# Seven block products for pairs of pooled gates, the layer input normalised again in place, and sums of weights formed by DMA

## Chip, core and metric

The kernel runs on one core of a Trainium2 chip. The metric is the device time of one execution in microseconds; several executions are taken and their median stands for the kernel. The engines of the core are TensorE (PE, the matmuls; PEld is its weight load), VectorE (DVE), ScalarE (ACT), GpSimd (POOL) and SyncE (SP), which issues most DMAs. Each engine works through its own queue in order; semaphores tie the queues together.

## What is computed

A decoder trunk with two layers (`DEPTH = 2`), 512 tokens and 16 learned meta tokens ahead of them (528 in all), model width 1024, in float32. Per layer, cut from the reference:

```python
h = rmsnorm(h_res, norm_gain[l])
proj = h @ w_in[l]
u_pool, z_pool, c_q, c_kv, k_rope, z_mla, g_pool, g_mla = jnp.split(proj, IN_SPLIT_POINTS, axis=-1)
y_pool = (pool_mix(u_pool, pool_w_group[l], pool_scale[l]) * jax.nn.silu(z_pool)) @ pool_w_up[l]
o_mla = mla(c_q, c_kv, k_rope, pos, ...)                 # 8 heads, causal, rotary parts, QK-norm
y_mla = (o_mla * jax.nn.silu(z_mla)) @ mla_w_up[l]
merged = jax.nn.sigmoid(g_pool) * y_pool + jax.nn.sigmoid(g_mla) * y_mla
h_res = h_res + merged @ w_out[l]
```

The change concerns `g_pool`, the pooled gate: a product of h (528 x 1024, in the last layer only the 512 tokens count) with 1024 columns of `w_in`, and beside it `g_mla` and `z_mla`, products of the same h.

## The kernel before

All activations lie transposed: channels on the 128 partitions, tokens in the columns. Each float32 product is made of three float32r matmuls on split operands (high x high, high weight x low input, low weight x high input), in `mm3` (L184 to L187). A split is a copy on ACT (high part) and a subtraction on DVE (low part): L276 and L277 for activations, L180 and L181 for weights.

**The stream of products.** `register` (L909) lists all products of a layer as `Gemm`s in order; `stream` (L193) runs through them in chunks of 512 weight columns (4 k-blocks), and has four chunks in preparation: the load by SP into `raw` (3 buffers), then `whi` and `wlo` (3 buffers each). In layer 0 a chunk serves two halves of 264 tokens, 24 matmuls; in layer 1 one piece of 512, 12 matmuls. Results come to PSUM (four buffers `mm`) and are evicted by the `ev_` functions.

**Order.** The list's order around the change: latent queries `cq`, pooled branch `u`, `zp`, `y`, heads' queries `qr`, `qn`, pooled projection `pu` (8), silu gate `zm` (4), pooled gate `gp` (8), attention's gate `gm` (8), attention's projection `mu` (8), output `o` (8). `go` (L973) sets what happens between: `qk_stats` forms the norms of queries (with the Newton steps of L283 to L290 and the factors `nqs`, L685), then the eight heads run. Each `head` (L715) makes scores (PSUM `S`, three buffers), a masked minimum on DVE (`top`, L730; the last of a head combines two halves, L764), exponentials on ACT (L737), and a normalisation on POOL (L774, L776); `pv` transposes and multiplies with the values (L796 to L802). `prep` (L694) makes the next head's key: a multiplication on DVE (L701) and one on POOL (L702), then a split; SP moves the rotary part of the query. Between these parts `gap` (L970) lets the stream advance by `FILL` ns of matmul time as the kernel counts it, until the product named in `RESERVE` is done: `pu`, `zm`, `gp`, and `gm` up to `gm5` fill PE between the attention tiles. The instruction order of each engine is then fixed by a scheduler at build time.

**Normalisation.** `split_h` (L332) splits x times the gain, without the token's factor 1/rms; that factor (`inv`, tile `rinv`) is multiplied in by each eviction: `ev_gp` (L570 to L577), `ev_gm` (L868 to L875), `ev_silu` (L499 to L509) for `zp` and `zm`. The split input stands in 16 tiles `hh`, `hl` all layer long. The tables of the rotary angles (`tcos`, `tsin`) stand in two tiles of their own.

Of the kernel before, what the change touches and what calls it, by code (L numbers as in the profile page):

```python
# [52 lines left out]
FILL = (2950.0, 2850.0)  # L53
RESERVE = ("gm5", "gm5")
# [17 lines left out]
def trunk(ctx, tc, xT, pos, win, wkr, wqb, wkb, wvb, wgr, wpu, wmu, wout, gains, const, yT):  # L72
# [81 lines left out]
    tcos = cp.tile([P, T], F32, name="tcos")  # L154
    tsin = cp.tile([P, T], F32, name="tsin")
# [6 lines left out]
    class Gemm:  # L162
        def __init__(self, name, src, width, evac=None, xs=None, segs=None, body=None, gain=None):
            self.name, self.src, self.width, self.alloc = name, src, width, mmt
            self.evac, self.xs, self.segs, self.body, self.gain = evac, xs, segs, body, gain
            self.spare = False

# [16 lines left out]
    def mm3(out, wh, wl, xh, xl, start, stop):  # L184
        pe.matmul(out, wh, xh, start=start, stop=False)  # L185
        pe.matmul(out, wh, xl, start=False, stop=False)  # L186
        newest[0] = pe.matmul(out, wl, xh, start=False, stop=stop)  # L187
# [5 lines left out]
    def stream():  # L193
# [3 lines left out]
        def load(i):  # L197
            g_, c = flat[i]
            n = min(512, g_.width - c)
            return wload(g_.src[:, c:c + n], n, g_.gain, g_.spare)  # L200
# [73 lines left out]

    def split(hi, lo, src, a, b):
        act.activation(hi[:, a:b], src, AF.Copy)  # L276
        dve.tensor_sub(lo[:, a:b], src, hi[:, a:b].bitcast(F32))  # L277
# [14 lines left out]
    def tables():  # L292
# [7 lines left out]
        dve.tensor_scalar(ang, ang, 3.1415925, -3.1415925, op0=ALU.min, op1=ALU.max)  # L300
        act.activation(tcos, ang, AF.Sin, scale=0.5)
        act.activation(tsin, ang, AF.Sin)
        dve.tensor_mul(tcos, tcos, tcos)
        dve.tensor_scalar(tcos, tcos, -2.0, 1.0, op0=ALU.mult, op1=ALU.add)

# [3 lines left out]
    kdr = [dp.tile([H, T], F32, name=f"kdr{l}") for l in range(DEPTH)]  # L309

    hbuf = [(slot(f"hh{k}", F32R), slot(f"hl{k}", F32R)) for k in range(8)]

    class Layer:
        def __init__(self, l):
            self.l, self.last = l, l == DEPTH - 1
            self.XS = XTOK if self.last else FULL
            self.x0 = NM if self.last else 0
            self.xt = xt if l == 0 else [None] * 8
# [7 lines left out]
            self.sq = []  # L326
            self.st = self.acc = self.inv = self.cinv = self.kraw = self.kp = None
# [154 lines left out]
        def rope(self, out, src, a, b):  # L482
# [3 lines left out]
            dve.tensor_mul(t[:, :n], t[:, :n], tsin[:, a:b])  # L486
            gp.tensor_mul(src, src, tcos[:, a:b])
# [11 lines left out]
        def ev_silu(self, dst, tag, m):  # L499
            def ev(ps, a, b):  # L500
                if a == self.x0:
                    dst[m] = slot(f"{tag}{m}") if tag == "u" else xb[:, m]
# [6 lines left out]
            return ev  # L509

# [59 lines left out]
        def ev_gp(self, m):  # L570
            def ev(ps, a, b):
                t = tmp()
                dve.tensor_mul(t[:, :b - a], ps, self.inv[:, a:b])
                act.activation(t[:, :b - a], t[:, :b - a], AF.Tanh, scale=0.5)
                dve.scalar_tensor_tensor(out=self.am[m][:, a:b], in0=t[:, :b - a], scalar=1.0,
# [534 lines left out]
```

## Time and profile before

| | us |
|---|---|
| median of 3 runs | 789.78 (789.15 to 790.03) |
| profiled execution, span from first to last instruction | 787.1 |
| busy in it: PE / DVE / ACT / POOL | 780.9 / 535.1 / 410.8 / 194.4 |
| layer 0's statistics of queries and keys on PE end (time in the span) | 155.0 |
| first scores of layer 0's head 1 | 190.2 |
| layer 1's statistics end | 550.6 |

The profile is of one execution. Line numbers are those of the kernel. A row of a view that groups instructions gives the line, the engine, the operation, output and inputs with their shapes, the count, then busy time in us and the mean of one in ns, then the engine's idle time before them and what ended it. A row of a timeline gives start and duration in us. A row by stage gives the stretch, its length, the busy time of each engine with the number of instructions, the granted clock of PE, the busy share of the DMA engines and GB/s.

### The profile page before, as it was taken

Reading aid. Unit: us, or ns where it says so; the run is one execution under the profiler, and the core shown is the slowest. Engines: PE = TensorE matmul, PEld = TensorE weight load, DVE = VectorE, ACT = ScalarE, POOL = GpSimd, SP = SyncE. Lnnn points to the kernel's source line nnn. Section 1 sums busy time; section 2 is a strip of 40 time slices with the busy share of each in tenths; the row PEclk is TensorE's granted clock in tenths of the full one; section 3 lists DMA queues with packets and bytes.
Section 4 is the critical chain, followed back from the end, with each engine's and each line's share of the span. In section 5 each row is a group of like instructions: output and inputs, shape, how many; then the busy total and the mean of one; then the engine's idle time right before and its main releaser. Section 6 shows DMA issues by size and latency. Waiting matters only on the chain.

```text
span 787.1 us, 14567 instructions
## 1 busy us (share of the span) xinstructions
PE 780.9 (99%) x5301; PEld 708.6 (90%) x5301; DVE 535.1 (68%) x1165; ACT 410.8 (52%) x930; POOL 194.4 (25%) x259
## 2 busy tenths in 40 slices
PE   9999999999999999999999999999999999999998
PEld 8999899999999999999997898887788888887887
DVE  5848787446779987675464487775467888755932
ACT  7645655635656565633354356455445666554420
POOL 1034504002333242051000145131022333410500
PEclk9999999999999999999999999999999999999999
DMA  6242333423223212224642422334232222122372
GB/s 242 82 102 85 96 120 102 128 81 94 96 76 92 78 58 78 95 81 146 192 123 94 95 88 90 129 88 136 96 105 88 95 84 82 65 81 67 102 242 84
DMA packets 52263, 81.83 MB, mean 104 GB/s; under 512 B 8784, under 2 KB 17360, under 8 KB 52192
## 3 DMA queue, kind: packets, MB, share of 16 engines
q1 hardware_dynamic: 52048, 80.65, 32.9%
q8 instruction: 41, 0.67, 0.4%
q14 instruction: 30, 0.25, 0.1%
q10 hardware_dynamic: 144, 0.26, 0.1%
HBM read 74.49 MB, written 4.27 MB: 100 GB/s over the span
## 4 chain that ended last, share of the span: by engine, by line
PE 95%; DMA 2%; DVE 1%; issue 1%; ACT 0%; SPq 0%; ACTq 0%
PE mm L185 28%; PE mm L187 28%; PE mm L186 28%; PE mm L796 2%; PE S L186 2%; PE S L187 1%; PE S L185 1%; PE o L802 1%; PE o L801 1%; PE S L453 1%; DMA xb<-xT 1%; PE mm L355 1%; DVE wlo L181 1%; PE mm L412 0%; DMA rinv<-win 0%
## 5 line engine op out<-in xcount | busy, mean ns | idle before, releaser
L185 PE MATMUL mm<-hh,whi 128*128 128x264 f32 (+2 forms) x1096 | 346.7, 318 | 0.2 <-ACT racc L810 0.2
L186 PE MATMUL mm<-hl,whi 128*128 128x264 f32 (+2 forms) x1096 | 343.9, 315 | 0.0
L187 PE MATMUL mm<-hh,wlo 128*128 128x264 f32 (+2 forms) x1096 | 343.0, 315 | 0.0
L181 DVE TENSOR_TENSOR wlo<-raw,whi 128x512 fp32r<-128x512 f32 (+2 forms) x251 | 188.6, 755 | 119.6 <-ACT whi L180 115.9
L180 ACT ACTIVATE whi<-raw 128x512 fp32r<-128x512 f32 (+2 forms) x251 | 150.4, 601 | 187.5 <-PE mm L186 126.5
L185 PEld LDWEIGHTS mm<-hh,whi 128*128 128x128 f32 x1096 | 205.9, 188 | 13.6 <-ACT racc L810 0.5
L186 PEld LDWEIGHTS mm<-hl,whi 128*128 128x128 f32 x1096 | 206.6, 189 | 11.8
L187 PEld LDWEIGHTS mm<-hh,wlo 128*128 128x128 f32 x1096 | 205.5, 188 | 12.0
L774 POOL TENSOR_TENSOR pm<-pa,rs 128x16 f32<-128x16 f32 x32 | 11.6, 361 | 181.3 <-DVE rs L769 181.3
L560 POOL TENSOR_TENSOR racc<-racc,tmp 128x264 f32<-128x264 f32 (+1 forms) x15 | 14.2, 948 | 153.8 <-ACT tmp L559 129.8
L702 POOL TENSOR_TENSOR tmp<-kp,bc 64x528 f32<-64x528 f32 x16 | 22.5, 1408 | 76.9 <-PE mm L675 44.5
L884 POOL TENSOR_TENSOR tmp<-tmp,xb 128x264 f32<-128x264 f32 (+1 forms) x24 | 27.1, 1149 | 58.2 <-DVE tmp L882 33.1
L730 DVE CUSTOM_DVE_ANT_0 S<-S,maskw,nqs 128x272 f32<-128x272 f32 (+4 forms) x80 | 38.5, 498 | 4.2 <-PE S L187 3.9
L737 ACT ACTIVATE cq<-S,bia 128x400 f32<-128x400 f32 (+2 forms) x48 | 24.6, 516 | 22.6 <-DVE bia L764 12.0
L185 PE MATMUL mm<-u,whi 128*128 128x264 f32 (+1 forms) x108 | 35.2, 326 | 0.0
L187 PE MATMUL mm<-cq,wlo 128*128 128x264 f32 (+1 forms) x108 | 34.5, 323 | 0.7 <-DVE wlo L181 0.7
L187 PE MATMUL mm<-u,wlo 128*128 128x264 f32 (+1 forms) x108 | 34.8, 323 | 0.0
L185 PE MATMUL mm<-cq,whi 128*128 128x264 f32 (+1 forms) x108 | 34.6, 320 | 0.0
L186 PE MATMUL mm<-cq,whi 128*128 128x264 f32 (+1 forms) x108 | 34.5, 321 | 0.0
L277 DVE TENSOR_TENSOR tl<-mm,th 128x512 fp32r<-128x512 f32 (+1 forms) x64 | 29.3, 481 | 6.1 <-ACT th L276 5.1
L776 POOL TENSOR_TENSOR cq<-cq,rs 128x384 f32<-128x384 f32 (+1 forms) x32 | 32.8, 1025 | 0.0
L186 PE MATMUL mm<-kn,whi 128*128 128x264 f32 (+1 forms) x96 | 30.7, 321 | 0.0
(252 smaller groups left out, 1362.4 us busy)
## 6 DMA issues: line engine op xcount, KB each, us to landing
raw<-win SPq DMA_DIRECT2D x143, 256.0 KB, 2.6
raw<-wout SPq DMA_DIRECT2D x32, 256.0 KB, 2.7
bc<-kdr SPq DMA_DIRECT2D x16, 264.0 KB, 3.6
raw<-wpu SPq DMA_DIRECT2D x16, 256.0 KB, 2.7
raw<-wmu SPq DMA_DIRECT2D x16, 256.0 KB, 2.5
raw<-wqb SPq DMA_DIRECT2D x12, 256.0 KB, 2.6
tmp<-xT SPq DMA_DIRECT2D x16, 132.0 KB, 3.0
tmp<-scr SPq DMA_DIRECT2D x7, 256.0 KB, 3.4
```

The source lines that it names most:

```text
L180: act.activation(hi[:, :n], raw[:, :n], AF.Copy)
L181: dve.tensor_sub(lo[:, :n], raw[:, :n], hi[:, :n].bitcast(F32))
L185: pe.matmul(out, wh, xh, start=start, stop=False)
L186: pe.matmul(out, wh, xl, start=False, stop=False)
L187: newest[0] = pe.matmul(out, wl, xh, start=False, stop=stop)
L277: dve.tensor_sub(lo[:, a:b], src, hi[:, a:b].bitcast(F32))
L702: gp.tensor_mul(kf[r0:r0 + 64, :], self.kp[r0:r0 + 64, :], bc[r0:r0 + 64, :])
L730: dve.tensor_tensor_reduce(out=sv, in0=sv, in1=mask, scale=nqs[:, i, h:h + 1], scalar=3e38, op0=ALU.add, op1=ALU.min, accum_out=bia[:, c:c ...
L737: act.activation(pv, sv, AF.Exp, scale=-1.0, bias=bia[:, i:i + 1], accum_out=rs[:, c:c + 1])
L776: gp.tensor_mul(pt[i][:, NM:], pt[i][:, NM:], rs[:, i:i + 1].to_broadcast([P, n - NM]))
L796: pe.transpose(tr[:, P * (i - j):P * (i - j + 1)], pt[i][:, NM + P * j:NM + P * (j + 1)], ident)
L884: gp.tensor_add(t[:, :b - a], t[:, :b - a], self.am[m][:, a:b])
```

## The change

Pairs of pooled gates are computed by seven block products instead of eight (a scheme of Strassen's kind, in Winograd's form): the 1024 inputs are halved into k-blocks 0 to 3 and 4 to 7, the tokens into two halves, the two gates of a pair are the two column blocks. `fast` makes seven products of 4 k-blocks for one half of the tokens, and its evictions add and subtract them. For this:

- `renorm` replaces the split input by the split of x times gain times `inv`, after the queries are done, so that the products give the gate without a factor; `ev_gm` and `ev_zm` lose their multiplication by `inv` (the factor 0.5 of `zm` moves to where it is used). It is called at eight points of `qk_stats`, 1500 ns of stream apart, in place of one filling of 9500.
- `mixed` forms four sums of halves of the input in place and splits them; its 16 calls stand at four places of each head, 8 of them do something.
- `weight_sums` copies weight blocks from HBM to HBM (`wsum`) on SP and adds others on top by accumulating DMAs that GpSimd issues; `stream` loads the sums like weights. Ten calls stand before head 0 and in heads 0 to 3.
- In the list, pairs `gp0` to `gp3` stand among `gm0` to `gm7`; `FILL` is 2770 and 2700 (2950 and 2850), `RESERVE` is `gp3`.
- For room, the first six `gm` gates are stored to HBM and loaded again (`gates_again`), and so are the rotary tables.

```diff
-FILL = (2950.0, 2850.0)
-RESERVE = ("gm5", "gm5")
+FILL = (2770.0, 2700.0)
+RESERVE = ("gp3", "gp3")
...
-    tcos = cp.tile([P, T], F32, name="tcos")
-    tsin = cp.tile([P, T], F32, name="tsin")
+    tab = [slot("tc"), slot("ts")]
...
+        def renorm(self, k):
...
+            f = self.f[k] = slot("sv", bufs=2) if k % 4 == 3 else slot(f"cq{k}")
+            f, (hh, hl), x0 = f[:, self.x0:T], self.hs[k], self.x0
+            x = xb[:, k, x0:T]
+            if k < 4:
+                sp.dma_start(f, scr[:, k, :] if self.last else xT[:, k, :])
+                x = f
+            behind(dve.scalar_tensor_tensor(out=f, in0=x, scalar=self.g(G_H + k), in1=self.inv[:, x0:T],
+                                            op0=ALU.mult, op1=ALU.mult), newest[0])
+            split(hh, hl, f, self.x0, T)
+
+        def mixed(self, i):
+            k, s = divmod(i, 2)
+            if k > 3:
+                return
+            (a, b), (_, c) = self.XH
+            n = b - a
+            u, w = self.f[k], self.f[k + 4]
+            if s == 0:
+                dve.tensor_sub(w[:, b:c], u[:, b:c], w[:, b:c])
+                dve.tensor_sub(u[:, b:c], u[:, a:b], u[:, b:c])
+                dve.tensor_sub(u[:, a:b], u[:, a:b], w[:, b:c])
+                dve.tensor_sub(w[:, a:b], w[:, a:b], u[:, a:b])
+                return
...
+            split(th, tl, u[:, a:c], a, c)
+            for h_, l_, v in ((t3h, t3l, w[:, b:c]), (t4h, t4l, w[:, a:b])):
+                split(h_, l_, v, 0, n)
...
+        def fast(self, name, a, b, u, got):
+            order = (1, 6, 7, 5, 2, 4, 3)
...
+            src = {1: a[:, 0:512], 2: a[:, 512:1024], 4: b[:, 512:1024], 5: s[:, 0, :], 6: s[:, 1, :], 7: s[:, 2, :],
+                   3: s[:, 3, :]}
...
+                for k in range(4):
+                    xh, xl = (x[:, t[0]:t[1]] for x in self.hs[k + o]) if p < 4 else self.tt[k][p]
+                    c = P * k
+                    mm3(ps, w[0][:, c:c + P], w[1][:, c:c + P], xh, xl, k == 0 and p not in (2, 4, 3), k == 3, True)
...
+                if p == 1:
+                    act.activation(d, ps, AF.Copy)
+                elif p == 6:
+                    dve.tensor_sub(d, d, ps)
+                elif p == 7:
+                    dve.tensor_sub(v, ps, d)
+                elif p == 5:
+                    dve.tensor_sub(v, v, ps)
+                    got(2 * u + 1, B, v, v)
+                elif p == 2:
+                    got(2 * u, A, ps, tmp()[:, :n])
+                elif p == 4:
+                    x = tmp()[:, :n]
+                    dve.tensor_sub(x, ps, d)
+                    got(2 * u + 1, A, x, x)
+                else:
+                    dve.tensor_add(d, d, ps)
+                    got(2 * u, B, d, d)
...
+        def weight_sums(self, i, w):
+            l = self.l
+            u, s = divmod(i, 2)
+            if u < 4:
+                a, b = w[2 * u], w[2 * u + 1]
+                d = wsum[l][u]
+                if s == 0:
+                    for i, t in enumerate((b[:, 0:512], a[:, 0:512], a[:, 0:512], a[:, 512:1024])):
+                        behind(sp.dma_start(d[:, i, :], t), newest[0])
+                else:
+                    for i, t in ((0, b[:, 512:1024]), (2, b[:, 0:512])):
+                        behind(gp.dma_start(d[:, i, :], t, accum_op=ALU.add), newest[0])
+            if 0 < u < 5:
+                d = wsum[l][u - 1]
+                behind(gp.dma_start(d[:, 3 if s else 1, :], d[:, 1 if s else 0, :], accum_op=ALU.add), newest[0])
...
-            fill_now(9500)
+            start = clk[0]
+            for i, k in enumerate((4, 5, 6, 7, 0, 1, 2, 3)):
+                self.renorm(k)
+                fill_to(start + 1500 * (i + 1))
...
-                    self.gms[m] = slot(f"cq{m}")
-                d = self.gms[m][:, a:b]
-                dve.tensor_mul(d, ps, self.inv[:, a:b])
-                act.activation(d, d, AF.Tanh, scale=0.5)
+                    self.gms[m] = slot(f"cq{m}" if m > 5 else "ts" if m % 2 else "tc")
+                act.activation(self.gms[m][:, a:b], ps, AF.Tanh, scale=0.5)
+                if m < 6 and b == T:
+                    sp.dma_start(gate[self.l][:, m, self.x0:T], self.gms[m][:, self.x0:T])
...
-            for m in range(8):
-                add(f"gp{m}", wi(MT_GP + m), D, evac=self.ev_gp(m), xs=hs, segs=XS)
-            for m in range(8):
-                add(f"gm{m}", wi(MT_GM + m), D, evac=self.ev_gm(m), xs=hs, segs=XS)
+            for e in ("gm0", "gp0", "gm1", "gm2", "gp1", "gm3", "gm4", "gp2", "gm5", "gp3", "gm6", "gm7"):
+                m = int(e[2])
+                if e[:2] == "gp":
+                    self.fast(e, wi(MT_GP + 2 * m), wi(MT_GP + 2 * m + 1), m, self.got_gp)
+                else:
+                    add(e, wi(MT_GM + m), D, evac=self.ev_gm(m), xs=hs, segs=XS)
...
-            fill_now(2600)
+            bit()
             kq = self.prep(0)
             fill_now(2600)
+            bit()
...
             for h in range(H):
-                kn_ = self.head(h, kq, prev)
+                kn_ = self.head(h, kq, prev, lambda: self.mixed(next(mix)))
                 self.gap()
+                self.mixed(next(mix))
+                bit()
                 if h + 1 < H:
                     kq = self.prep(h + 1)
                 self.pv(prev, (2, 3))
+                bit()
+                self.mixed(next(mix))
                 prev = kn_
                 self.gap()
+                self.mixed(next(mix))
...
             self.pv(prev, (2, 3))
+            up("gm6")
+            self.gates_again()
             up("gm7")
```

More of the change, by code (lines that the diff above doesn't have):

```diff
@@ L273, in fill_now, with fill_to @@
             pass
+    def fill_to(end):
+        while clk[0] < end and step():
+            pass
     def split(hi, lo, src, a, b):
@@ L755, in head @@
             self.gap()
+            between()
             self.pv(prev, (0, 1))
@@ L975, in go, with bit @@
             up = lambda name: upto((l, name))
+            made, mix = iter(range(99)), iter(range(99))
+            def bit():
+                i = next(made)
+                if i < 10:
+                    self.weight_sums(i, [win[l, MT_GP + m] for m in range(8)])
             if l == 0:
```

108 lines of the change are left out of this document (84 added, 24 removed).

## The prediction

> **What bounds the kernel now.** I read the page first (span, engines, chain), then rows of TensorE's timeline, then busy time by stage, then VectorE's instructions by form.
>
> ```profile
> span 787.1 us, 14567 instructions
> ...
> PE 780.9 (99%) x5301; PEld 708.6 (90%) x5301; DVE 535.1 (68%) x1165; ACT 410.8 (52%) x930; POOL 194.4 (25%) x259
> PEclk9999999999999999999999999999999999999999
> ...
> PE 95%; DMA 2%; DVE 1%; issue 1%; ACT 0%; SPq 0%; ACTq 0%
> ```
> The page: TensorE (PE) is busy for 780.9 of 787.1 us, its clock is granted in full in all slices, and 95% of the chain that ended last is PE. So the time follows the number of matmuls and what one costs, as long as nothing keeps them waiting. The span is 787.1 us; the runs' median, 789.78 us, lies 2.7 us above it, and I keep that difference.
>
> How far apart matmuls start, in timeline rows (start, duration): layer 0's merge (59 rows from the first to the last), layer 1's output projection (36 rows), and its last tile in 256-column halves (41 rows).
>
> ```profile
> 344.83 0.28 PE L186 MATMUL mm<-kn,whi 128*128 128x264 f32 x1
> ...
> 351.90 0.28 PE L187 MATMUL mm<-q,wlo 128*128 128x264 f32 x1
> ```
>
> ```profile
> 739.81 0.39 PE L185 MATMUL mm<-hh,whi 128*128 128x512 f32 x1
> ...
> 747.89 0.39 PE L186 MATMUL mm<-hl,whi 128*128 128x512 f32 x1
> ```
>
> ```profile
> 778.78 0.28 PE L186 MATMUL mm<-hl,whi 128*128 128x256 f32 x1
> ...
> 783.51 0.28 PE L187 MATMUL mm<-hh,wlo 128*128 128x256 f32 x1
> ```
> 58 steps in 7.07 us are 121.9 ns for 264 columns; 35 in 8.08 us are 230.9 ns for 512; 40 in 4.73 us are 118.3 ns for 256. The 0.28 and 0.39 us are latencies that overlap.
>
> The engine with the next least room is VectorE (DVE). By stage (columns: stretch, its length, then busy time of PE, PE's weight loads, DVE, ACT, POOL), the heads of layer 0:
>
> ```profile
> 190.00:320.00 130.00, 130.00 (x1062) 128.50 (x1061) 106.14 (x258) 77.07 (x199) 42.51 (x68) 1.00 0.25 79
> ```
> 106.14 of 130 us: 82%, in the stage into which the change puts its work.
>
> **The change: what PE saves.** A pair of pooled gates was, per layer 0, 2 tiles x 8 k-blocks x 3 x 2 halves = 96 matmuls of 264 columns; seven block products of 4 k-blocks x 3 are 84. Over four pairs that is 48 x 121.9 ns = 5.9 us. In layer 1 it was 2 x 8 x 3 = 48 of 512 columns, and becomes 84 of 256: 4 x (48 x 230.9 - 84 x 118.3) ns = 4.6 us. Sum: **10.4 us** off PE, if nothing waits. No other matmul is added or lost.
>
> **What VectorE gets.** Durations by form (count, then busy us, mean ns):
>
> ```profile
> L181 DVE TENSOR_TENSOR wlo<-raw,whi 128x512 fp32r<-128x512 f32 x223 | 175.0, 787 | 111.5 <-ACT whi L180 110.0
> ...
> L277 DVE TENSOR_TENSOR kl<-tmp,kh 128x528 fp32r<-128x528 f32 x16 | 11.6, 726 | 4.9 <-ACT kh L276 4.8
> ...
> L338 DVE SCALAR_TENSOR_TENSOR hl<-xb,gn,hh 128x528 fp32r<-128x528 f32 x15 | 10.9, 764 | 4.0 <-ACT hh L336 4.0
> ...
> L575 DVE SCALAR_TENSOR_TENSOR xb<-tmp,xb 128x264 f32<-128x264 f32 x16 | 7.3, 457 | 0.8 <-ACT tmp L574 0.8
> ...
> L573 DVE TENSOR_TENSOR tmp<-mm,rinv 128x264 f32<-128x264 f32 x16 | 6.7, 424 | 0.3
> ```
> I take 0.79 us for a 512-wide low part of a weight, 0.73 for a 528-wide one, 0.76 for a 528-wide scaling, 0.44 for anything of 264. Per layer: `renorm` adds 8 scalings and 8 low parts (8 x 1.49 = 11.9); `mixed` adds 16 subtractions of 264 and low parts of 4 x 528 and 8 x 264 (7.0 + 2.9 + 3.5 = 13.4); products use a weight chunk for half as many columns, so 28 chunks instead of 16 (12 x 0.79 = 9.5); the pair's evictions are 9 instructions instead of 8 (1.8); the gates `gm` lose their multiplication by `inv` (16 x 0.44 = 7.0) and `zm` one of two (3.5). Sum for layer 0 about 26 us, for layer 1 much the same: about 52 us on 535. That is hidden only where DVE has room.
>
> **The stretch where it has none: layer 0, from the statistics to head 1's scores.** In the trace DVE sums the statistics from 155.48, takes head 0's last minimum (L764) at 186.55, and PE starts head 1's scores at 190.16:
>
> ```profile
> 155.48 0.89 DVE L464 TENSOR_TENSOR tmp<-S,tmp 8x264 f32<-8x264 f32 x2 [1.30 <-ACT tmp L463]
> 156.84 0.71 DVE L277 TENSOR_TENSOR kl<-tmp,kh 128x528 fp32r<-128x528 f32 x1 [0.47 <-ACT kh L276]
> 157.95 0.69 DVE L181 TENSOR_TENSOR wlo<-raw,whi 128x512 fp32r<-128x512 f32 x1 [0.40 <-ACT whi L180]
> ...
> 183.05 0.43 DVE L505 SCALAR_TENSOR_TENSOR u<-mm,rinv 128x264 f32<-128x264 f32 x1
> ...
> 186.55 0.15 DVE L764 TENSOR_TENSOR bia<-bia 128x1 f32<-128x1 f32 x1
> ```
>
> ```profile
> 190.16 0.29 PE L185 MATMUL S<-kh,qhl 128*128 128x272 f32 x1
> ```
>
> ```profile
> 155.48:186.55 31.07, 31.07 (x256) 30.64 (x255) 16.55 (x44) 14.14 (x33) 1.33 (x1) 1.00 0.28 86
> 155.48:190.16 34.68, 34.68 (x285) 34.25 (x284) 19.55 (x53) 17.11 (x43) 2.40 (x5) 1.00 0.33 98
> ...
> 551.00:583.00 32.00, 32.00 (x148) 25.82 (x147) 16.64 (x41) 13.16 (x26) 1.32 (x1) 1.00 0.27 90
> ```
> DVE is busy for 16.55 us up to that minimum; PE needs 34.68 us to head 1's scores. In the built order of the changed kernel, DVE's queue holds all 8 scalings and 8 low parts of `renorm`, all 16 subtractions, the low parts of all four `mixed` sums (12 instructions), one more `kl` and 2 more weight chunks ahead of that same minimum, with the Newton steps of `nqs` between them: 11.9 + 13.4 + 0.73 + 1.6 = 27.6 us more, 44.2 in all. With the lengths of the undisturbed rows above (0.69 to 0.71 us for 512 to 528 columns, 0.43 for 264) it is 43.0. PE has 280 matmuls before head 1's first scores, where it had 285: 34 us. The scores need the banks that head 0's exponentials free, and those wait for the minimum. So PE comes 9 to 10 us early; some 70 matmuls stand before the last score that waits, against another 7 us of DVE, which leaves 8. Queued behind the minimum on DVE are `kl` of head 2 and every later weight's low part, and on PE the fill matmuls stand behind the waiting scores, so nothing can be drawn forward. I take **8 us**; from below 0 (if DVE catches up out of sight), from above 11.
>
> **Layer 1, the same stretch.**
>
> ```profile
> 550.94 0.88 DVE L464 TENSOR_TENSOR tmp<-S,tmp 8x248 f32<-8x248 f32 x2 [1.13 <-ACT tmp L463]
> ...
> 584.19 0.14 DVE L764 TENSOR_TENSOR bia<-bia 128x1 f32<-128x1 f32 x1
> ```
>
> ```profile
> 587.61 0.29 PE L185 MATMUL S<-kh,qhl 128*128 128x272 f32 x1
> ```
> 16.64 us busy between 551 and 583, the minimum at 584.19, head 1's scores at 587.61, 36.7 us after 550.94. With some 26 us more DVE needs 43. Here the built order leaves 165 matmuls of 512 columns before head 1's scores (38.1 us), with 2.6 us of others 40.8. I take **2 us**, between 0 and 6.
>
> **The products among the heads.** A chunk of 12 matmuls lasts 1.46 us on PE where one of 24 lasted 2.93. It needs a high part on ACT, then a low part on DVE:
>
> ```profile
> L180 ACT ACTIVATE whi<-raw 128x512 fp32r<-128x512 f32 x223 | 139.8, 629 | 174.0 <-PE mm L186 122.4 <-issue 20.3 <-PE mm L187 10.1
> ```
> 0.63 + 0.79 = 1.42 us in a row, with three buffers. A pair is 84 x 0.122 = 10.2 us on PE and 7 x 0.79 + 9 x 0.44 = 9.5 on DVE, before any of the heads' own DVE work. A run of seven therefore only fits because the `gm` gates between ask for 1.6 us of DVE in 5.9 (layer 0). Eight runs at 0 to 1 us: **2.5 us**.
>
> **Queues.** SP's gets 92 more issues on 377: 24 weight chunks, 32 copies from HBM to HBM, and the sources of `f`, the tables and six stored gates with their way back. Each copy stands ahead of weights and is held until a named matmul has run. POOL's gets 32 accumulating DMAs among its multiplications for the next head's key (L702):
>
> ```profile
> L702 POOL TENSOR_TENSOR tmp<-kp,bc 64x528 f32<-64x528 f32 x16 | 22.5, 1408 | 76.9 <-PE mm L675 44.5 <-issue 20.2 <-DVE xb L575 11.9
> ```
>
> ```profile
> raw<-win SPq DMA_DIRECT2D x143, 256.0 KB, 2.6
> ```
> A load of 256 KB lands 2.6 us after issue, and the weights are 3 to 4 chunks ahead (4.4 us at least), so four copies in front of a load cost nothing unless they take over about 4 us more. No accumulating DMA is in this trace; by the load's row one lands in about 2.6 us, and a copy, its accumulation and the one on top of it follow each other: some 8 us, asked for a head before the first product that reads them. The reload of the gates, on SP ahead of `gm6`'s second chunk, has the last three products of gp3 and half of `gm6` as cover, 60 matmuls or 7.3 us; without them, a landing of about 2.6 us. I take **0.5 us** for all queues, between 0 and 8.
>
> Sum: 787.1 - 10.4 + 8 + 2 + 2.5 + 0.5 = 789.7 us of span, with 2.7 around it **792.4 us**.
>
> [...] Two forms of one line, from PSUM and from SBUF:
>
> ```profile
> L277 DVE TENSOR_TENSOR tl<-mm,th 128x512 fp32r<-128x512 f32 x16 | 11.0, 686 | 2.7 <-ACT th L276 2.7
> ...
> L277 DVE TENSOR_TENSOR hl<-tmp,hh 128x512 fp32r<-128x512 f32 x8 | 7.1, 906 | 1.1 <-ACT hh L276 0.9
> ```
> 686 ns against 906 for the same 512 columns; the second form reads two SBUF operands while POOL adds in the merge. [...] All of `renorm` and `mixed` has two SBUF inputs. [...]
>
> **Rivals.** (1) *The saving stays*: the backlog on DVE decides. It rests on the minimum standing last in the queue, and on 43 us of work. If the scores need less of head 0 than I think, or DVE keeps closer to PE, so that all places together lose less than 10.4 us, the kernel is faster. For it, a stretch in which DVE is busy for 15.97 of 16.34 us and PE for all of it:
>
> ```profile
> 262.57:278.91 16.34, 16.34 (x133) 16.21 (x132) 15.97 (x38) 10.73 (x28) 4.27 (x8) 1.00 0.24 79
> ```
> With 2 to 4 us lost: 789.8 - 10.4 + 3 = 782.4.
>
> (2) *GpSimd's queue*: the key of head 2 stands in POOL's queue behind accumulations that wait for copies, which wait for a matmul of head 0. If a copy or an accumulation takes three times the 2.6 us, head 2's scores come 7 us later than in my sum, in layer 0 or in both: 799 to 806. For it: nothing in the trace bounds these DMAs. Against: DMA engines are busy for 25% in this stage. [...]
>
> **How the numbers follow.** Forecast, DVE's backlog takes back what PE saves and a little more: 0.52, 787 to 797. Rival 1: 0.28, 779.5 to 786. Rival 2: 0.15, 797 to 808. Rival 3: 0.05. The range reaches to rival 1 and to the nearer part of rival 2: 781 to 802. A difference under 0.2% (1.6 us) can't be told from none here. Faster, below 788.2: rival 1 and a little of the forecast, 0.31. Within: 0.16. Slower, above 791.4: 0.53.
>
> **What would show it.** PE's matmuls 96 more in number; steps of 118 and 122 ns in the products; DVE about 585 us busy. A gap on PE of 5 to 10 us between the statistics and head 2's scores in layer 0, released by DVE or by ACT behind it, with DVE's busy time near 100% of some 50 us: right. Gaps there under 3 us: rival 1, and my price of the backlog is wrong. Gaps released by POOL's key product or by DMAs into `wsum`: rival 2. It would also be wrong if weights arrive late (ACT idle until DMA `raw`), or if 256-column products cost more than 118 ns.

## The result: 824.8 us, 4.6% slower, and the profile after

| | before | after |
|---|---|---|
| median | 789.7 us (789.15 to 790.03, 4 runs) | 824.8 us (823.6 to 829.4, 4 runs) |
| ratio to before, 95% interval | | 1.0456 (1.0428 to 1.0484) |
| profiled execution, span | 787.1 us | 821.9 us |
| PE busy / matmuls | 780.9 us / 5301 | 790.0 us / 5397 |
| mean granted clock of PE | 1.000 | 0.981 |

The forecast was 792.4 us, 781 to 802. The page of the changed kernel, the rows that answer to those of before, and its DMA rows (queue: packets, MB, share of the 16 engines' span; then issues with KB and median us from issue to landing):

```profile
span 821.9 us, 15208 instructions
...
PE 790.0 (96%) x5397; PEld 719.0 (87%) x5397; DVE 579.5 (71%) x1265; ACT 440.7 (54%) x1010; POOL 224.6 (27%) x291
...
PE   9999999997988999899999999999997989999998
...
PEclk9999999998899999999999999999998899999999
...
q1 hardware_dynamic: 65296, 104.93, 41.9%
q0 software_dynamic: 4608, 8.39, 7.1%
...
raw<-win SPq DMA_DIRECT2D x135, 256.0 KB, 2.9
wsum<-win SPq DMA_DIRECT2D x32, 256.0 KB, 6.6
...
wsum<-win POOLq DMA_DIRECT2D x16, 256.0 KB, 7.4
wsum<-wsum POOLq DMA_DIRECT2D x16, 256.0 KB, 6.9
```
PE has 96 matmuls more, as it should, and DVE 579.5 us of work (forecast 585). New are holes in PE's row and slices in which its clock is not granted in full. PE is idle for 31.9 us of the span (6.2 before), and with a mean clock of 0.981 some 1.9% of 821.9, 15.6 us, went to a slower clock.

The first hole, by stage (stretch, length, busy us of PE, PEld, DVE, ACT, POOL, clock, DMA share, GB/s):

```profile
180.00:190.00 10.00, 10.00 (x84) 10.00 (x83) 9.94 (x26) 7.97 (x20) 1.72 (x2) 1.00 0.69 152
190.00:200.00 10.00, 6.42 (x53) 6.22 (x52) 5.78 (x16) 3.02 (x9) 3.74 (x4) 1.00 1.03 258
200.00:210.00 10.00, 7.50 (x33) 6.81 (x34) 8.23 (x27) 6.17 (x22) 4.95 (x10) 0.54 0.44 119
```
Before, PE was busy throughout these 30 us and the DMA engines for 20% of 190 to 200. Now they are full (1.03; the share adds up the packets' times, so it can pass 1), and from 196.4 to 198.9 us PE, DVE and ACT all stand still. PE's rows at the hole, then ACT's and DVE's:

```profile
196.14 0.27 PE L191 MATMUL S<-kh,qhl 128*128 128x240 f32 x1
200.57 0.49 PE L187 MATMUL S<-kh,qhl 128*128 128x400 f32 x1 [4.16 <-ACT cq L872]
```

```profile
198.89 0.63 ACT L182 ACTIVATE whi<-raw 128x512 fp32r<-128x512 f32 x1 [5.15 <-DMA raw<-win]
199.43 0.65 ACT L539 ACTIVATE tmp<-mm 128x264 f32<-128x264 f32 x2
199.97 0.46 ACT L872 ACTIVATE cq<-S,bia 128x240 f32<-128x240 f32 x1
```

```profile
195.18 0.16 DVE L900 TENSOR_TENSOR bia<-bia 128x1 f32<-128x1 f32 x1
199.55 0.69 DVE L183 TENSOR_TENSOR wlo<-raw,whi 128x512 fp32r<-128x512 f32 x1 [4.22 <-ACT whi L182]
```
Read one after the other: PE waits for an exponential of ACT (L872). That needs head 0's last minimum (L900), which DVE had done by 195.4. But ACT took the exponential only at 199.97: ahead of it in its queue stands a weight's high part (L182), which waited 5.15 us for its load. So the releaser named at PE is not the cause; the load is. In the window from 190 to 200 us the view of DMA issues gives:

```profile
raw<-win SPq DMA_DIRECT2D x3, 256.0 KB, 8.0
wsum<-win POOLq DMA_DIRECT2D x2, 256.0 KB, 7.4
```
A load that took 2.6 us before lands after 8.0. And behind the hole the clock falls, from 1.00 to 0.50 (microsecond by microsecond):

```profile
199.00:200.00 1.00, 0.00 (x0) 0.00 (x0) 0.45 (x1) 1.00 (x4) 0.00 (x0) 1.00 1.12 223
200.00:201.00 1.00, 0.43 (x2) 0.43 (x3) 1.00 (x3) 1.00 (x6) 0.00 (x0) 0.92 0.94 174
201.00:202.00 1.00, 1.00 (x7) 0.81 (x6) 1.00 (x6) 1.00 (x5) 0.00 (x0) 0.50 0.84 195
210.00:211.00 1.00, 1.00 (x6) 1.00 (x6) 0.00 (x0) 0.13 (x2) 1.00 (x5) 0.50 0.00 0
211.00:212.00 1.00, 1.00 (x10) 1.00 (x9) 0.00 (x0) 0.00 (x0) 1.00 (x4) 0.96 0.00 0
```
From 201 to 211 us the clock is 0.50: a gap of 4.2 us, then 10 us at half speed, with another gap of 1.8 us in them.

### The profile page after: what moved, and what is told of

It is laid out like the page before. It is cut to its first block, busy times and chain, and to the rows that moved or that the text cites. A ratio compares the mean times of both kernels' runs of the same rounds, so it can differ in the third digit from the quotient of the medians.

```text
span 821.9 us, 15208 instructions
## 1 busy us (share of the span) xinstructions
PE 790.0 (96%) x5397; PEld 719.0 (87%) x5397; DVE 579.5 (71%) x1265; ACT 440.7 (54%) x1010; POOL 224.6 (27%) x291
## 5 line engine op out<-in xcount | busy, mean ns | idle before, releaser
L187 PE MATMUL mm<-hh,whi 128*128 128x264 f32 (+2 forms) x1000 | 313.3, 316 | 3.0 <-ACT whi L182 1.2
L191 PE MATMUL mm<-hh,wlo 128*128 128x264 f32 (+2 forms) x1000 | 311.1, 314 | 0.8 <-DVE wlo L183 0.8
L190 PE MATMUL mm<-hl,whi 128*128 128x264 f32 (+2 forms) x1000 | 311.1, 312 | 0.0
L183 DVE TENSOR_TENSOR wlo<-raw,whi 128x512 fp32r<-128x512 f32 (+2 forms) x275 | 205.3, 750 | 127.8 <-ACT whi L182 116.3
L182 ACT ACTIVATE whi<-raw 128x512 fp32r<-128x512 f32 (+2 forms) x275 | 165.7, 605 | 212.9 <-PE mm L190 130.5
L187 PE MATMUL mm<-cq,whi 128*128 128x264 f32 (+2 forms) x172 | 53.7, 312 | 1.4 <-DVE tl L285 1.4
L191 PE MATMUL mm<-cq,wlo 128*128 128x264 f32 (+2 forms) x172 | 53.1, 311 | 0.7 <-DVE wlo L183 0.7
L190 PE MATMUL mm<-cq,whi 128*128 128x264 f32 (+2 forms) x172 | 53.0, 309 | 0.0
L865 DVE CUSTOM_DVE_ANT_0 S<-S,maskw,nqs 128x288 f32<-128x288 f32 (+4 forms) x80 | 38.4, 499 | 2.6 <-PE S L191 2.3
L187 PEld LDWEIGHTS mm<-cq,whi 128*128 128x128 f32 x172 | 32.9, 191 | 3.1 <-DVE tl L285 1.6
L191 PEld LDWEIGHTS mm<-cq,wlo 128*128 128x128 f32 x172 | 32.9, 192 | 2.6 <-DVE wlo L183 1.1
L187 PE MATMUL S<-kh,qhl 128*128 128x272 f32 (+5 forms) x88 | 25.3, 303 | 9.6 <-ACT cq L872 8.2
L190 PEld LDWEIGHTS mm<-cq,whi 128*128 128x128 f32 x172 | 33.0, 192 | 1.7
```

What stands on the lines that cost most here:

```text
L182: act.activation(hi[:, :n], raw[:, :n], AF.Copy)
L183: dve.tensor_sub(lo[:, :n], raw[:, :n], hi[:, :n].bitcast(F32))
L187: first = pe.matmul(out, wh, xh, start=start, stop=False, skip_group_check=more)
L190: pe.matmul(out, wh, xl, start=False, stop=False, skip_group_check=more)
L191: newest[0] = pe.matmul(out, wl, xh, start=False, stop=stop, skip_group_check=more)
L865: dve.tensor_tensor_reduce(out=sv, in0=sv, in1=mask, scale=nqs[:, i, h:h + 1], scalar=3e38, op0=ALU.add, op1=ALU.min, accum_out=bia[:, c:c ...
```

## The experiments

Three theories. **1**: the transfers for the weights' sums fill the DMA engines and weights come late. **2**: VectorE's backlog from `renorm` and `mixed`, the forecast. **3**: the order of SP's and POOL's queues, whatever the transfers move. Medians, with the ratio to the kernel before on the same chip (789.4 to 790.1 us):

| run | what differs | us | ratio (95%) |
|---|---|---|---|
| no_sums | changed kernel without the sums' DMAs | 800.6 | 1.0128 (1.0109 to 1.0147) |
| thin_sums | the sums' DMAs with 1/8 of the bytes | 802.0 | 1.0163 (1.0126 to 1.0200) |
| before_sums | kernel before with the sums' DMAs | 798.7 | 1.0109 (1.0091 to 1.0128) |
| early_sums | changed, sums spread one by one | 809.4 | 1.0250 (1.0233 to 1.0267) |
| copies_only | changed, no accumulating DMAs | 804.1 | 1.0183 (1.0160 to 1.0205) |
| no_sums_no_spill | no_sums, gates not stored | 797.4 | 1.0097 (1.0076 to 1.0118) |
| no_sums_light | no_sums without renorm and mixed | 788.6 | 0.9986 (0.9972 to 1.0000) |
| no_sums_light_no_spill | both | 787.4 | 0.9970 (0.9959 to 0.9981) |
| light_sums | changed without renorm and mixed | 813.1 | 1.0287 (1.0264 to 1.0310) |
| light_sums_deep | the same, 5 weight buffers | 791.3 | 1.0032 (1.0011 to 1.0052) |
| no_sums_light_deep | no_sums_light, 5 weight buffers | 787.2 | 0.9975 (0.9963 to 0.9986) |
| after_deep | changed kernel, up to 5 buffers | 811.4 | 1.0287 (1.0260 to 1.0314) |
| last_only | change in layer 1 alone | 796.5 | 1.0085 (1.0061 to 1.0109) |
| last_in_heads | the same, sums in layer 0's heads | 791.9 | 1.0030 (1.0018 to 1.0041) |
| stalls | before, with VectorE held up four times | 802.3 (one run) | |

**Is it the transfers?** no_sums:

```diff
-                if i < 10:
+                if i < 0:
                     self.weight_sums(i, [win[l, MT_GP + m] for m in range(8)])
...
-            src = {1: a[:, 0:512], 2: a[:, 512:1024], 4: b[:, 512:1024], 5: s[:, 0, :], 6: s[:, 1, :], 7: s[:, 2, :],
-                   3: s[:, 3, :]}
+            src = {1: a[:, 0:512], 2: a[:, 512:1024], 4: b[:, 512:1024], 5: b[:, 0:512], 6: a[:, 0:512], 7: a[:, 512:1024],
+                   3: b[:, 512:1024]}
```


> The weights' sums are left out: no copies and no accumulating DMAs, and products 5, 6, 7 and 3 load plain columns of the same size (so the pooled gates come out of other weights). All else stands, renorm, mixed and the order of the list among it. If the DMA engines are what holds the weights up (theory 1), the stalls and the half clock go and the saving of 10.4 us shows: 778 to 787 us. If VectorE's backlog holds PE (theory 2, the forecast's term of 13 us), nothing that matters has gone: 812 to 825. If SP's and POOL's queues hold it by their order (theory 3), 778 to 787 as well; this run does not tell 1 from 3.

800.6: 24.2 us go, so theory 1 or 3 has most of the loss; but it is no saving, so 2 has a part as well.

**Bytes or order?** thin_sums:

```diff
-behind(sp.dma_start(d[:, i, :], t), newest[0])
+behind(sp.dma_start(d[0:16, i, :], t[0:16]), newest[0])
```
The accumulations are shortened in the same way; a load of a sum takes its other partitions from plain columns.

> Every copy and every accumulating DMA stays at its place, with its waits, but moves 16 of 128 partitions, an eighth of the bytes; a load of a sum takes these 16 partitions from the sum and the other 112 from plain columns, as two DMAs (so the gates are not the reference's). Theory 1 (the DMA engines' time): most of the loss goes, 780 to 790 us. Theory 3 (the order of the queues, the issue time of 0.8 us on POOL, the chain of copy, accumulation and load): 810 to 825. Theory 2 (VectorE): 812 to 825.

802.0, though all 64 DMAs, their waits and POOL's issue time are there (POOL busy for 227.3 us). That ends theory 3 as it was put, whatever the transfers move: their volume counts. My numbers for theory 1 (780 to 790) were too low since the part of theory 2 was left out of them.

**Which of the transfers?** copies_only:

```diff
-                else:
-                    for i, t in ((0, b[:, 512:1024]), (2, b[:, 0:512])):
-                        behind(gp.dma_start(d[:, i, :], t, accum_op=ALU.add), newest[0])
-            if 0 < u < 5:
-                d = wsum[l][u - 1]
-                behind(gp.dma_start(d[:, 3 if s else 1, :], d[:, 1 if s else 0, :], accum_op=ALU.add), newest[0])
```

> The changed kernel with the 32 copies on SP, but without the 32 accumulating DMAs on GpSimd's queue: the four summed blocks are plain copies (so the gates are others). Of the DMA engines' extra time the accumulations are some 58 us and the copies some 30. If the price goes by the engines' time: 806 to 811 us, two thirds of the 24 us gone. If the copies, which stand in SP's queue ahead of weights, are what counts: 816 to 822.

804.1: taken away in this order, the copies cost 3.5 us and the accumulations 20.7. I had expected two thirds; they have six sevenths.

**The transfers by themselves:** before_sums puts `weight_sums` and its ten calls into the kernel before.

```diff
             fill_now(2600)
+            bit()
             kq = self.prep(0)
             fill_now(2600)
+            bit()
...
                 self.gap()
+                bit()
                 if h + 1 < H:
                     kq = self.prep(h + 1)
                 self.pv(prev, (2, 3))
+                bit()
```

> The kernel before, with the same 32 copies and 32 accumulating DMAs at the same ten calls, into tensors that nothing reads; no products of seven, no renorm, no mixed. Theory 1: the DMA engines fill in both layers' heads and weights come late here too: 800 to 825 us. Theory 2: VectorE has no more to do, 789 to 793. Theory 3: the key's multiplication waits on POOL's queue and loads behind copies on SP's: 795 to 815.

798.7: 9.3 us. That is just under theory 1's range and far from 24, and it lies inside theory 3's. One matmul of layer 0's attention projection that waits for the merge, in the kernel before and in this one:

```profile
338.75 0.39 PE L185 MATMUL mm<-q,whi 128*128 128x264 f32 x1 [0.28 <-DVE tmp L882]
```

```profile
339.15 0.39 PE L185 MATMUL mm<-q,whi 128*128 128x264 f32 x1 [0.28 <-DVE tmp L900]
```
Layer 0 loses 0.4 us to the very transfers that tear holes into the changed kernel; nearly all the rest of this execution's 7.7 us is lost around one hole in layer 1, with the clock falling around it (0.81 in the mean from 610 to 615 us, 0.51 from 615 to 620). That hole runs through GpSimd's queue:

```profile
603.67 0.17 DVE L787 RECIPROCAL rs<-rs 128x4 f32<-128x4 f32 x1
```

```profile
606.99 0.83 POOL L524 DMA_DIRECT2D wsum<-win  x1 [6.28 <-DVE bia L748]
607.87 0.22 POOL L792 TENSOR_TENSOR pm<-pa,rs 128x16 f32<-128x16 f32 x1
```

```profile
610.36 0.31 ACT L807 ACTIVATE pmr<-pm 128x128 fp32r<-128x128 f32 x1 [6.08 <-POOL pm L792]
```
The factors of a head's normalisation (`rs`) are ready at 603.8. The normalisation starts at 607.9, since an accumulating DMA stands ahead of it in POOL's queue, and ACT, in whose queue weights stand as well, waits for it. In the program the accumulation waits only for a matmul and for its copy. The four copies were issued from 599.5 on and took 8.3 us (median) to land, so it is probably the copy and not the named DVE that ends this wait; that is argued, not shown. Theory 3 is thus not out: with transfers of full size, POOL's order passes a slow landing on to work that has nothing to do with it.

By themselves the transfers cost well under half of the 24 us; the changed kernel is more sensitive to them.

**Sensitive through VectorE's backlog?** light_sums drops the call of `renorm` and makes `mixed` hand out plain halves.

```diff
-                self.renorm(k)
...
+            (h0, l0), (h1, l1) = self.hs[k], self.hs[k + 4]
...
+            self.tt[k] = {6: (h0[:, a:b], l0[:, a:b]), 5: (h0[:, b:c], l0[:, b:c]),
+                          7: (h1[:, b:c], l1[:, b:c]), 4: (h1[:, a:b], l1[:, a:b])}
```

> The changed kernel with renorm and mixed taken out (its products read plain halves of the split input, so the gates are others), and with all 64 DMAs for the sums where the change puts them. Without the sums this kernel took 788.6 us. If the transfers cost what they cost in the changed kernel whatever VectorE does (24 us): 811 to 815. If their price there comes from both together, because a VectorE that is behind frees the raw buffers late, loads then start late and a landing of 8 us reaches PE: nearer to what they cost the kernel before (9 us): 795 to 802.

813.1, against 788.6 without the sums: 24.5 us, with VectorE relieved. So the total does not need the backlog. The largest hole, between 230 and 241 us, among the first products, again has a late load in its chain (waits; us in total, times, longest), and then a subtraction on VectorE (a timeline row, and the stretch beside it):

```profile
PE o L920 <- DVE tmp L936: 8.4, 1, 8.4
...
ACT whi L182 <- DMA raw<-win: 5.5, 1, 5.5
DVE wlo L183 <- ACT whi L182: 4.7, 1, 4.7
```

```profile
236.36 4.03 DVE L183 TENSOR_TENSOR wlo<-raw,whi 128x512 fp32r<-128x512 f32 x1 [4.67 <-ACT whi L182]
```

```profile
235.00:240.00 5.00, 0.00 (x0) 0.00 (x0) 3.64 (x1) 4.08 (x10) 4.92 (x11) 0.59 0.99 164
```
What PE waits for (L936) stands behind that subtraction in VectorE's queue. The subtraction takes 0.69 us in the changed kernel (median of 275) and 4.03 here, beside multiplications of GpSimd, which is busy for 4.92 of these 5 us. So the late load is not all of this hole. What the stretched row has to do with GpSimd no run separates.

**Through the lead of the weights?** light_sums_deep and its control let loads take two more buffers among the heads:

```diff
     def rawt():
+        turn[0] += 1
+        if more[0] and turn[0] % 5 > 2:
+            return slot(f"cq{turn[0] % 5 - 3}")
         return wp.tile([P, 512], F32, tag="raw", name=nm("raw"), bufs=3)
```


> As light_sums (813.1 us: the sums' transfers kept, renorm and mixed out), with five buffers for loaded weights among the heads where there were three. A chunk of a product feeds 1.46 us of matmuls where a gate's feeds 2.93, so three loads in flight cover 4.4 us where they covered 8.8, and a landing takes 8 us while sums are formed; five cover 7.3. If the sums cost 24 us here and 9 in the kernel before because of that lead: 795 to 804. If the DMA engines are simply full and weights come as late with any number of buffers: 809 to 814.

> The same five buffers without the sums, as a control beside no_sums_light (788.6 us). If the lead matters only while the sums are formed: 787 to 790. If what the products still lose (8 us of the 10.4) is late weights too: 781 to 786.

791.3 and 787.2: with five buffers the same 64 transfers cost 4.1 us, with three 24.5. 791.3 is below both my ranges. Its ten runs reach from 789.4 to 796.2, and the profiled one is among the lowest. Between 215 and 245 us, where light_sums had its hole, transfers still take long to land:

```profile
raw<-win SPq DMA_DIRECT2D x3, 256.0 KB, 4.3
wsum<-wsum POOLq DMA_DIRECT2D x3, 256.0 KB, 6.5
raw<-wsum SPq DMA_DIRECT2D x3, 256.0 KB, 6.2
...
wsum<-win POOLq DMA_DIRECT2D x2, 256.0 KB, 8.4
```
and PE hardly sees it any more:

```profile
PE 774.9 (98%) x5397; PEld 708.0 (90%) x5397; DVE 541.1 (69%) x1177; ACT 421.8 (54%) x970; POOL 223.3 (28%) x291
...
PEclk9999999999999999999999999999999999999999
```
So in this kernel neither full engines nor late landings decide by themselves, but landing time against lead: three loads in flight cover 3 x 2.93 = 8.8 us of a gate's matmuls, but 3 x 1.46 = 4.4 us of a product's.

**In the changed kernel itself**, after_deep moves `zm2` and `zm3` behind the first two pairs, and their slots hold weights until then (fewer extra buffers than above, and for a part of the time).

```diff
+EXTRA = {"gm0": ["u2", "u3"], "zm2": ["u3"], "zm3": []}
...
+        turn[0] += 1
+        i = turn[0] % (3 + len(extra[0])) - 3
+        if i >= 0:
+            return slot(extra[0][i])
...
-            for e in ("gm0", "gp0", "gm1", "gm2", "gp1", "gm3", "gm4", "gp2", "gm5", "gp3", "gm6", "gm7"):
+            for e in ("zm0", "zm1", "gm0", "gm1", "gm2", "gp0", "zm2", "gp1", "zm3", "gm3", "gm4", "gp2", "gm5", "gp3",
+                      "gm6", "gm7"):
```

> The changed kernel with all its parts, and up to five buffers for loaded weights while the sums are formed: zm2 and zm3 move behind the first two pairs of gates (with gm1 and gm2 ahead of gp0), and their two slots hold weights until then. If the shorter lead of the weights is what the sums' transfers break: most of 24 us gone, 801 to 812. If not: 818 to 828. Renorm's and mixed's 12 us stay in either case, so it does not come under the kernel before.

811.4, at the upper end: 13.5 of the 24 us come back. The order of the list changes with the buffers here, and no run separates the two.

The first hole of the changed kernel, the one shown above, is not explained by the shorter lead. At 196 us the stream is still at `zm`, whose chunks feed 24 matmuls as before; the first product's eviction comes at 230.57. after_deep, whose extra buffers are in use by then, still has a gap of 2.83 us at the same score. There ACT waits for no load but for the next key's multiplication on POOL (L844, which starts at 196.71), and that stands behind accumulating DMAs, one of which waited for the other's landing:

```profile
194.98 0.81 POOL L652 DMA_DIRECT2D wsum<-wsum  x1 [3.66 <-DMA wsum<-wsum]
```

```profile
198.03 0.64 ACT L292 ACTIVATE kh<-tmp 128x528 fp32r<-128x528 f32 x1 [1.40 <-POOL tmp L844]
```

```profile
199.17 0.45 PE L194 MATMUL S<-kh,qhl 128*128 128x400 f32 x1 [2.83 <-ACT cq L880]
```
light_sums has no gap at this place, with the same transfers and the DMA engines as full:

```profile
195.00:200.00 5.00, 5.00 (x43) 4.96 (x42) 3.36 (x6) 2.98 (x8) 2.95 (x3) 1.00 1.05 271
```
Without the sums the same score waits 0.74 us (no_sums). So this hole takes the transfers together with `renorm` and `mixed`, and the 24.2 us of the changed kernel and the 24.5 of light_sums are made up of different holes; that they agree so well is chance.

**What is left without the sums.** no_sums_light and two with the spilled gates taken out (merges 0 to 5 use gates 4 and 5); the gates' edit, the other is that of light_sums:

```diff
-                if m < 6 and b == T:
-                    sp.dma_start(gate[self.l][:, m, self.x0:T], self.gms[m][:, self.x0:T])
...
-                self.gms[m] = slot(f"cq{m}")
-                sp.dma_start(self.gms[m][:, self.x0:T], gate[self.l][:, m, self.x0:T])
+                self.gms[m] = self.gms[4 + m % 2]
```

> As no_sums (800.6 us), with renorm and mixed taken out: the products read plain halves of the split input (so the gates are those of other inputs, and without the factor inv). VectorE loses some 25 us of work a layer, ScalarE some 15, at the places where both stand now. Theory 2 (VectorE's backlog carries what is left when the sums are gone, 21 us above 779): 784 to 792. Rivals: chunks used for half as many columns, PSUM banks held by a pair, the spilled gates: 796 to 802.

> As no_sums (800.6 us), and the six attention gates are neither stored nor loaded again: the merge uses gates 4 and 5 for gates 0 to 5 (that part of the computation is changed). Theory: at the end of layer 0's heads, where no_sums lost some 6 us between 321 and 332 us, the stores keep SP waiting for their gate (4.8 us at the longest) and six reloads of 264 KB come in front of weights: 793 to 796. Rival: the weights are late there because VectorE is: 798 to 802.

> Both: as no_sums without renorm and mixed, and without store and reload of gates. What remains of the change is the seven products, their evictions and the order of the list. If the account is complete, the saving of 10.4 us shows: 778 to 782 us. If products among the heads cost by themselves (chunks, banks, evictions): 783 to 795.

788.6: `renorm` and `mixed` cost 12.0 us. Spilling the gates costs 3.2 us beside them, less than my range for it had, and 1.2 without them, which the intervals hardly tell from nothing. What then remains of the change, 787.4, still lacks 8 of the 10.4 us. Of the 8.5 us that its span lacks, 5.7 are idle time of PE (11.9 us of 785.2, where it was 6.2 before); the waits that the profile names there are on ACT and DVE, none longer than 1.2 us. The control with five buffers gained 1.4 us on no_sums_light, within the intervals, so late loads are not shown to be it. Why the products lose this time among the heads stays open.

Where the 12.0 us fall, by PE's first score of head 5 and the first matmul of the attention projection in layer 0, in no_sums and in no_sums_light:

```profile
258.23 0.34 PE L187 MATMUL S<-kh,qhl 128*128 128x272 f32 x1
...
344.03 0.39 PE L187 MATMUL mm<-q,whi 128*128 128x264 f32 x1 [0.41 <-ACT q L284]
```

```profile
250.71 0.34 PE L187 MATMUL S<-kh,qhl 128*128 128x272 f32 x1
...
332.12 0.39 PE L187 MATMUL mm<-q,whi 128*128 128x264 f32 x1 [0.43 <-ACT q L284]
```
7.5 us by head 5, 11.9 by the projection; the spans differ by 13.1, so layer 1 has 1.2. In no_sums DVE has no room in the first stretch (155.5 to 196 us, columns as above):

```profile
155.50:196.00 40.50, 40.50 (x334) 39.66 (x327) 38.24 (x94) 26.33 (x60) 2.83 (x2) 1.00 0.33 101
```
38.2 of 40.5 us, and 20.8 of 39.5 in no_sums_light.

**Does the place of the transfers matter?** early_sums and last_only pop the 64 (32) DMAs one by one as the stream advances; last_in_heads moves them. The popping in `step`, and the edit from last_only to last_in_heads (layer, first, every ns):

```diff
+        while sums and sums[0][0] <= clk[0]:
+            sums.pop(0)[3]()
         c = next(main, None)
...
-((1, 30000.0, 12000.0),)
+((1, 150000.0, 2700.0),)
```


> The changed kernel with the same 64 DMAs for the sums, spread one by one: layer 0's every 5.5 us of the stream from 14 us on, layer 1's every 8 us from 215 us on, so each layer's sums are done before its products begin. Theory 1: the engines never fill, 780 to 790 us, faster than before by a little or equal. Theory 2: 812 to 825. Theory 3: POOL's multiplications for keys no longer stand behind accumulations that wait: 780 to 795.

> Layer 0 as in the kernel before; the change in layer 1 alone, with its sums spread one by one every 12 us of the stream from 30 us on. The saving is then 4.6 us. The DMA theory: 32 transfers over some 400 us hold nothing up; with layer 1's own loss of some 5 us in no_sums, 788 to 791. If the transfers hold up weights one by one wherever they stand: 793 to 799.

> As last_only (796.5 us: the change in layer 1 alone), with layer 1's 32 transfers one by one every 2.7 us of the stream among the heads of layer 0, instead of from 30 us on. In the kernel before layer 0's heads took such transfers at a price of 0.4 us, while last_only lost 5 us ahead of 175 us, where weights come at a quicker pace. By the place: 788.5 to 792. If a transfer costs the same wherever it stands: 795 to 798.

809.4 misses all its ranges: it is 8.8 us above no_sums, where I had counted neither the 12 us of renorm and mixed nor a price for spread transfers. 796.5 lies where the dearer theory had it, and 791.9, with the transfers closer together, shows that it is the place. last_only starts layer 0's scores at 180.69 us and last_in_heads at 176.81; for layer 1's scores it is 582.44 and 576.44, and the difference stays near 6 to the end. So transfers ahead of the heads cost time, and among layer 0's heads, which have no products in these two runs, they cost little. The saving of layer 1 alone, 4.6 us, is eaten there too: 791.9 is 1.9 us above the kernel before on the same chip. No version that forms the sums came out under the kernel before.

**What a hole costs.** stalls repeats a weight's subtraction on VectorE at four weights.

```diff
+HELD = {115: 14, 121: 18, 242: 22, 248: 16}
...
+        for _ in range(HELD.get(loads[0], 0)):
+            dve.tensor_sub(lo[:, :n], raw[:, :n], hi[:, :n].bitcast(F32))
         dve.tensor_sub(lo[:, :n], raw[:, :n], hi[:, :n].bitcast(F32))
```

> The kernel before, with VectorE held up ahead of the low part of four weights in the two output projections, by 14, 18, 22 and 16 repeats of the same subtraction (9.7, 12.4, 15.2 and 11 us of VectorE). It asks what one stall of PE costs in all. [...]

802.3, 12.2 us above the kernel before on the same chip (790.1). That is under the 815 to 835 that I had put down, an estimate whose price of a hole no run shows. The holes also came out shorter than the 3 to 8 us that I had planned, the longest so:

```profile
758.69 0.50 PE L190 MATMUL mm<-hh,wlo 128*128 128x512 f32 x1 [2.17 <-DVE wlo L184]
```

```profile
756.00:758.00 2.00, 0.52 (x3) 0.09 (x1) 1.93 (x4) 0.49 (x1) 0.00 (x0) 1.00 0.48 158
758.00:760.00 2.00, 1.31 (x6) 1.10 (x7) 2.00 (x5) 0.00 (x0) 0.00 (x0) 1.00 0.22 39
```
This hole of 2.17 us leaves the clock at 1.00. What a longer one does to it, this run doesn't say.

## Why the prediction was wrong, by its steps

- **PE's saving**, 10.4 us: the matmul count is right (5397). Nothing showed it whole: the best variant, 787.2, has 2.5 of it.
- **DVE's work**, 585 us: right (579.5).
- **Backlog on DVE**, 8 us in layer 0's first stretch and 2 in layer 1: near in size, but not at the wait that was priced, so the nearness is luck. `renorm` and `mixed` cost 12.0 us, 11.9 of the spans' 13.1 in layer 0. VectorE was late as forecast: in no_sums head 0's last minimum starts at 195.56 us, 9.0 later than before, with 38 us of DVE's work up to it where 44 had been counted. But the scores of head 1 that wait behind it cost PE 0.74 us, not 8:

```profile
197.89 0.45 PE L187 MATMUL S<-kh,qhl 128*128 128x400 f32 x1 [0.74 <-ACT cq L872]
```
The loss comes at other waits, over heads 1 to 4 and at the heads' end, and through the clock: of the spans' 13.1 us, 7.6 are idle time of PE and 5.5 are PE's busy time, at a mean clock of 0.994 against 1.000. (The calls of `mixed` are 32, four a head; the eight that do something stand in heads 0 and 1.)

- **Products among the heads**, 2.5 us between 0 and 8: mis-sized. Without sums, renorm and mixed, 788.6 lies 9.3 us above the 779.3 that the whole saving gives (789.7 - 10.4); 1.2 of that may be the stored gates, which the prediction had under the queues.
- **Queues, "0.5 us, between 0 and 8"**: the step that failed. The sums' transfers cost 24.2 us. The argument was that four copies ahead of a load cost nothing "unless they take over about 4 us more". They did: 8.0 us to land where 2.6 was quoted. The lead of 4.4 us stood in the same sentence. Two more buffers for weights bring the price of the same transfers from 24.5 us to 4.1 in light_sums_deep, so it is the landing against the lead. The step took landing times from a stretch with room on the DMA engines and used them for one in which the change itself takes that room. The trace of before would have given an estimate: q1 moves 80.65 MB in 32.9% of 787.1 us, 259 us, so 256 KB take 0.84 us of all 16 engines. At a load's price 64 transfers are 54 us and 24 more loads 20 us, on two times some 100 us that were 28% full (165 to 270 us): some 65% in the mean, and more in the bursts of four copies. In the changed kernel it is 72% in the mean of 165 to 270 us, and over 1 in the bursts. The prediction's own sign of being wrong, ACT idle until a load has landed, is what the trace shows (5.15 us). By the releaser's name alone the hole would have passed for the forecast's, since PE waits for ACT there and DVE had been busy for 9.94 of the 10 us before 190.
- **Rival 2** had slow copies and accumulations, but their price through POOL's queue and the key. thin_sums shows that the queue's order costs next to nothing while the transfers are short; at full size before_sums has such a hole, in a normalisation, and in after_deep ACT waits 1.40 us for the key, as the rival had it. Its 799 to 806 was too small besides.
- **Rivals 1 and 3**: the saving did not stay, even without sums, renorm and mixed. Rival 3 was my estimate of a price on VectorE's instructions beside GpSimd's; no run shows it, since none changes GpSimd's work alone. Measured is one subtraction of 4.03 us in light_sums, against a median of 0.69 in the changed kernel, with GpSimd busy for 4.92 of 5 us beside it.
- **The clock** had no price in any term. Between no_sums (0.994) and the changed kernel (0.981), both with 5397 matmuls, PE's busy time differs by 10.4 us (779.6 and 790.0): of the 24 us, close to half is PE's work at a slower clock.

The account in medians: 789.7 - 10.4 + 9.3 (products and spills) + 12.0 (renorm, mixed) + 24.2 (sums) = 824.8. It closes by construction: the last three terms are read off as differences, which does not explain them.

## What to carry over

A transfer had two prices here: the engines' time that it took (256 KB: 1.8 us of all 16 for an accumulating DMA, 1.3 for a copy), which must be added up over the stage, and the landing time that it gave all the others (8.0 us for a load where 2.6 was the median before), which must be held against the lead of the tightest consumer (4.4 us, by estimate from 3 x 1.46). This change halved the matmul time per loaded block (2.93 to 1.46 us), and with it that lead; the same transfers cost 9.3 us in the kernel before, 24.5 in light_sums and 4.1 there with two more buffers. Look behind the releaser that a wait names, at what stood in that engine's queue ahead of the releaser: PE's wait of 4.16 us named an exponential of ACT, and ahead of that stood ACT's wait of 5.15 us for a load.

## What the runs showed of the hardware

- The 32 accumulating DMAs from HBM onto HBM took more of the DMA engines than the copies did: in the changed kernel their packets have 7.1% of 821.9 us on all 16 engines, 1.8 us each for 256 KB (2.0 in before_sums, 7.9% of 794.8 us); a copy (before_sums: q1 at 37.7% of 794.8 us against 32.9% of 787.1) has 1.3 us, and q1's traffic of before, taken by 256 KB, 0.84.
- In no_sums the clock fell to 0.50 by 326 us, and no gap of PE in the 5 us before was over 1.47: three gaps of 1.47, 0.43 and 0.85 us, with PE busy for 2.25 of 5 us, were followed by 6 us at half speed:

```profile
321.00:326.00 5.00, 2.25 (x16) 1.66 (x15) 2.44 (x6) 2.62 (x6) 0.00 (x0) 0.94 0.82 290
326.00:332.00 6.00, 6.00 (x28) 6.00 (x29) 2.51 (x6) 1.76 (x5) 0.00 (x0) 0.50 0.17 44
332.00:334.00 2.00, 2.00 (x15) 1.86 (x15) 0.00 (x0) 0.39 (x1) 0.00 (x0) 0.94 0.00 0
```
